# Four tiles for a mixer state, its sample load on GpSimd's queue, and two-instruction norms in a streaming encoder step

## The chip, the cores and the metric

The kernel runs on one core of one Trainium2 chip. The metric is the device time of one execution in microseconds (us). Before the change three runs took 1357.20, 1358.41 and 1359.65 us, so the median is 1358.41 us.

## What is computed

The reference is one step of a one-layer streaming encoder: 1024 frames of a new stream (the prompt) and 32 frames of a running stream (the sample), which brings its states along.

```python
def run_trunk(x, states, params):            # DEPTH = 1
    h, st_new = mixer(rms_norm(x, g_mix_pre), ...)   # GLA | HGRN2 | mLSTM heads, then cat @ w_out
    x = x + rms_norm(h, g_mix_post)
    h, ffn_buf = conv_ffn(rms_norm(x, g_ffn_pre), ...)   # gelu(gate) * val, D_FF = 2816
    x = x + rms_norm(h, g_ffn_post)
...
def rms_norm(x, g):
    y = xf * lax.rsqrt(jnp.mean(xf * xf, axis=-1, keepdims=True) + EPS)
...
    s_new = exp(b_last) * s + einsum('bjhk,bjhv->bhkv', kc * exp(b_last - b), vc)   # GLA and HGRN2, chunks of 64
```

D_MODEL is 1024, so a norm is over 1024 columns. For the prompt the states start at zero, for the sample they come from HBM (`s_gh` holds GLA's and HGRN2's matrices, 128x256, and `s_c` mLSTM's). The states after the last chunk are outputs too.

## The kernel before

The 1056 rows are nine **units**: u = 0 to 7 are 128 prompt rows each, and u = 8 is the sample's 32 rows. Each product in f32 is three TensorE matmuls of split operands (`mm3`, L101 to L103), so most TensorE rows come in threes with these lines.

The stages follow each other, and overlap at their edges:

1. The input norm and the in-projection (`pv` products), in three groups of units: 0 to 2, 3 to 5, 6 to 8. While one group is projected, the **mixers** of the group before it run piece by piece between the projection's pieces (`merge` and `pump`).
2. The mixers, in the order of units 0, 1, 2, 3, 4, 5, 8, 6, 7. A mixer makes scores (`sc`), masks them into `P` (DVE, L831), makes the outputs `og` and `oh` (heads of GLA and HGRN2) and `om` and `oi` (mLSTM) on TensorE, and `finish` (L1009 to L1019) norms them by head: ACT squares, DVE sums, GpSimd makes the reciprocal root (`hrs`), DVE multiplies it into `cat` (L1017), GpSimd multiplies the gate in (L1019).
3. The out-projection (`zp` products, by unit and half: `zp40` is unit 4, half 0), with the post norm, the residual and the FFN's pre norm (`outproj`). Its operands `ch` and `cl` are split from `ctp` transposes (L1105, L1106), and `fxt` transposes bring the normed rows into the FFN's layout (L1207, then `z` on DVE, L1212). The mixers of units 8, 6 and 7 run between the pieces of the out-projection of units 0 to 4 and 8.
4. The FFN's up products (`puw`, `pux`) and down products (`x`, `q`), by Strassen-like sums of blocks; weights such as `wu0r` and `wu22r` come by SP's queue and are split and summed in halves.
5. The tail: for units 0 to 3 the last down product `q` is added (`ca<-ca,q`, L1703), squared (ACT, L1578), multiplied by the gain (`ca<-ca,gp`, L1582), and two halves of `fr` (L1599) apply the post norm and the residual.

**The running state.** The states of GLA and HGRN2 lie in tiles of tag "S". A tag with `bufs=3` has three buffers that are handed out in turn: the fourth tile takes the first one's buffer, and whoever writes it first waits for the last reader of the tile that lay there. Unit 0 and unit 8 begin with a tile S (zeros, and for the sample a load from `s_gh`, L788); each chunk of 64 rows makes one more (L927): `S4_1` is the state of unit 4 behind its second chunk. Counting in order, S8 takes the buffer of S4_1 with three buffers; S4_1 is read by the first-chunk matmuls `og<-S` and `oh<-S` of unit 5.

```python
                sp.dma_start(S, a["s_gh"])                                   # L788
                Sn = mx.tile([128, 4, 64], F32, tag="S", ..., bufs=3)        # L927
                dve.tensor_tensor(Sn, S, dec[...]..., op=ALU.mult)           # L928
                si = dve.tensor_tensor(Sn, Sn, up, op=ALU.add)               # L929
```

**The norms over 1024 columns** come in halves. ACT squares each half and leaves its sum in one column; GpSimd adds the two columns (L1176 in `outproj`, L1585 in `down_all`), and `rstd_of` divides by 1024 and adds EPS (L221) and raises to the power −1/2 (L222): three instructions of 128x1. There are nine such norms in `outproj` (`oss`) and nine in `down_all` (`gss`). Only unit 0's input norm (L307, L308) makes two instructions of it, since its squares are taken of x/32.

**What sets the order.** Each engine works through its own queue in order. The queues are ordered at build time by the framework, which simulates the program with times of its own: an edit in one place moves instructions elsewhere that it has nothing to do with. `tc.high_priority` and `tc.issue_after` steer a few of them.

Of the kernel before, what the change touches and what calls it, by code (L numbers as in the profile page):

```python
# [8 lines left out]
F32 = mybir.dt.float32  # L9
# [3 lines left out]
AF = mybir.ActivationFunctionType  # L13
ALU = mybir.AluOpType
# [9 lines left out]
EPS = 1e-6  # L24
# [67 lines left out]
def body(ctx: ExitStack, tc: tile.TileContext, a: dict):  # L92
    nc = tc.nc
    act, dve, pool, pe, sp = nc.scalar, nc.vector, nc.gpsimd, nc.tensor, nc.sync
# [25 lines left out]
    mx = mxs.enter_context(tc.tile_pool(name="mx", bufs=1, side="left", reuse_waits="tile"))  # L120
# [37 lines left out]
    def const(name, shape, dt=F32, src=None):  # L158
        t = cp.tile(shape, dt, name=name)
        if src is not None:  # L160
            sp.dma_start(t, src)
        return t
# [29 lines left out]
    mhalf = const("mhalf", [128, 16])  # L192
# [26 lines left out]
    def rstd_of(out, ss, n, cols, width, eps=EPS):  # L219

        pool.tensor_scalar(out, ss, 1.0 / width, eps, op0=ALU.mult, op1=ALU.add)  # L221
        pool.tensor_tensor(out, out, mhalf[:n, :cols], op=ALU.pow)  # L222


    Ld = [mx.tile([128, 4, 128], F32, name=f"Ld{i}") for i in range(2)]
    Qz = [mx.tile([128, 6, 64], F32, name=f"Qz{i}") for i in range(2)]
    qz = mx.tile([128, 11, 128], F32, name="qz")
# [51 lines left out]
    def units_of(g):  # L279
        t0, pl, sl = GROUPS[g]  # L280
        us = [(t0 // 128 + i, 128 * i, 128) for i in range(pl // 128)]
        if sl:
            us.append((8, pl, sl))
        return us
# [8 lines left out]
    def scale_x(g):  # L293
        for (u, off, n) in units_of(g):
            x = x_in.pop(u, None)
            x = load_x(u) if x is None else x
            if g == 0:
                jk = mx.tile([128, 1024], BF16, tag=("gt", "cat", "k")[u], name=f"jk{u}", bufs=1)
            else:
                jk = mx.tile([128, 1024], BF16, tag="qe", name=f"jk{u}", bufs=1)  # L300
            rs = p1.tile([128, 1], F32, tag="rs", name=f"rs{u}", bufs=2)
            if u == 0:
                ss = p1.tile([128, 2], F32, name="ss0")
                hs = slice(0, 512), slice(512, 1024)
                for i, c in enumerate(hs):
                    act.activation(jk[:, c], x[:, c], AF.Square, scale=1.0 / 32, accum_out=ss[:, i:i + 1])
                pool.tensor_scalar(rs, ss[:, 0:1], ss[:, 1:2], EPS, op0=ALU.add, op1=ALU.add)  # L307
                pool.tensor_tensor(rs, rs, mhalf[:, :1], op=ALU.pow)  # L308
                for c in hs:
                    dve.scalar_tensor_tensor(x[:, c], x[:, c], rs, gx[:, c], op0=ALU.mult, op1=ALU.mult)  # L310
                xn_of[u] = x
                yield
                continue
            ss = p1.tile([128, 1], F32, tag="ss", name=f"ss{u}", bufs=2)
            with tc.issue_after(vgi[0].ins) if vgi else ExitStack():
                act.activation(jk[:n], x[:n], AF.Square, accum_out=ss[:n])
            rstd_of(rs[:n], ss[:n], n, 1, 1024)
            with tc.issue_after(vgi[1].ins) if vgi else ExitStack():
                dve.scalar_tensor_tensor(x[:n], x[:n], rs[:n], gx[:n], op0=ALU.mult, op1=ALU.mult)
            xn_of[u] = x  # L320
            yield
# [424 lines left out]
    def mixer(u, g, ci0):  # L746
        n = 128 if u < 8 else DEC
# [31 lines left out]


        if u in (0, 8):
            S = mx.tile([128, 4, 64], F32, tag="S", name=f"S{u}", bufs=3)
            C = mx.tile([128, 3, 65], F32, tag="C", name=f"C{u}", bufs=3)
            if u == 0:
                dve.memset(S, 0.0)
                dve.memset(C, 0.0)
            else:
                sp.dma_start(S, a["s_gh"])  # L788
                sp.dma_start(C, a["s_c"])
            state["S", u == 8], state["C", u == 8] = S, C  # L790

# [10 lines left out]
        with ExitStack() as behind:  # L802
            if halves:

                for ins in (kwi[0], halves[1]):
                    behind.enter_context(tc.issue_after(ins.ins))
            spread(dve, qz, lambda r, fs, psl: dve.tensor_tensor(qz[r, psl, :n], q4[r, fs, :], eb4[r, fs, :],
                                                                 op=ALU.mult), n)
# [73 lines left out]
        ss = mx.tile([128, 16], F32, tag="hss", name=f"hss{u}", bufs=2)  # L882
        rs = mx.tile([128, 16], F32, tag="hrs", name=f"hrs{u}", bufs=2)
# [31 lines left out]
        def states():  # L915
            si = None
            ups = []
            for ch, (o, m) in enumerate(chunks):
                up = small(4, 64)
                ups.append(up)  # L920
                for (f, r0, dk, vc) in HEADS:
                    soon(pe.matmul, up[r0:r0 + dk, f, :], kt2[:n, ch, 128 * f + r0:128 * f + r0 + dk], v[:n, vc:vc + 64],
                              start=True, stop=True)
            for ch, up in enumerate(ups):
                S = state["S", u == 8]
                Ss.append(S)
                Sn = mx.tile([128, 4, 64], F32, tag="S", name=f"S{u}_{ch}", bufs=3)  # L927
                dve.tensor_tensor(Sn, S, dec[:, :, ch:ch + 1].broadcast_to([128, 4, 64]), op=ALU.mult)  # L928
                si = dve.tensor_tensor(Sn, Sn, up, op=ALU.add)  # L929
                state["S", u == 8] = Sn  # L930
            return si
# [19 lines left out]
        for l0 in range(0, len(levels), 2):  # L951
            pair = [operands(c, i) for i, c in enumerate(levels[l0:l0 + 2])]
            last_pair = pair[-1][0] == levels[-1]
            if last_pair:
                z = mx.tile([128, 512], F32, tag="x", name=f"x{u}_0", bufs=NX)
# [125 lines left out]
    def outproj(p2, W, u):  # L1081

        gm, woh, wol = W[:3]
        n = 128 if u < 8 else DEC
# [6 lines left out]
        for hf in range(2):  # L1091
            if u < 7 or u == 8:
                ps = psb.tile([128, 4, 128], F32, tag="big", name=f"ctp{u}{hf}")
            else:
# [3 lines left out]
                ps = both[:, hf]  # L1098
# [3 lines left out]
            ch = p2.tile([128, 4, 128], F32R, tag="ch", name=f"ch{u}{hf}", bufs=3)  # L1102
# [15 lines left out]
        ss = pgm.tile([128, 4], F32, tag="oss", name=f"oss{u}", bufs=2)  # L1118
        cs = [slice(512 * hf, 512 * hf + 512) for hf in range(2)]
# [7 lines left out]

        def leave(ps, hf):

            act.activation(z[:n, cs[hf]], ps[:n], AF.Square, accum_out=ss[:n, hf:hf + 1])  # L1130
            act.copy(z[:n, cs[hf]], ps[:n])

        if u == RING[0]:

            pss = [bank(hf) for hf in range(2)]
            for k in range(8):
                next(W[3])
                for hf in range(2):
                    product(pss[hf], hf, k)
            z = ring[0](f"z{u}")  # L1140
            for hf in range(2):
                leave(pss[hf], hf)
            yield
        elif u in RING:

            z = ring[0](f"z{u}")
            for hf in range(2):
                ps = bank(hf)
                for k in range(8):
                    product(ps, hf, k)  # L1150
                leave(ps, hf)
                if not hf:
                    yield
        elif u == 6:
            pss = [bank(hf) for hf in range(2)]
            for k in range(8):
                for hf in range(2):
                    product(pss[hf], hf, k)
                if k == 3:
                    yield  # L1160
            z = tail[0](f"z{u}")
            for hf in range(2):
                leave(pss[hf], hf)
        else:

            pss = [bank(hf) for hf in range(2)]
            jk = jks[0]
            for hf in range(2):
                for k in range(8):
                    product(pss[hf], hf, k)  # L1170
                with tc.high_priority(offset=AHEAD):
                    kept["jk"] = act.activation(jk, pss[hf], AF.Square, accum_out=ss[:, hf:hf + 1])
        load_res(u)
        x = xr_of[u]
        yield
        pool.tensor_tensor(ss[:n, 2:3], ss[:n, 0:1], ss[:n, 1:2], op=ALU.add)  # L1176
        rstd_of(ss[:n, 3:4], ss[:n, 2:3], n, 1, 1024)
        if u == 7:
            for hf in range(2):
                dve.scalar_tensor_tensor(pss[hf], pss[hf], ss[:, 3:4], gm[:, cs[hf]], op0=ALU.mult, op1=ALU.mult)  # L1180
# [5 lines left out]
        if u == 7:  # L1186
            z = tail[0]("z7")
# [30 lines left out]
    upper, jks, kept, pgs = [], [], {}, ExitStack()  # L1218
# [314 lines left out]
    def down_all(ph, pc, begun, late):  # L1533
# [41 lines left out]

        def square_of(u, n, src, half, ss):
            jk = pc.tile([128, 512], BF16, tag="fjk", name=f"gjk{u}{half}", bufs=2)
            act.activation(jk[:n], src, AF.Square, accum_out=ss[:n, 2 + half:3 + half])  # L1578

        def norm_of(u, n, src, half, ss):  # L1580
            square_of(u, n, src, half, ss)
            dve.tensor_tensor(src, src, gp[:n, 512 * half:512 * half + 512], op=ALU.mult)  # L1582

        def scale_of(n, ss):
            pool.tensor_tensor(ss[:n, 0:1], ss[:n, 2:3], ss[:n, 3:4], op=ALU.add)  # L1585
            rstd_of(ss[:n, 1:2], ss[:n, 0:1], n, 1, 1024)

        def added(u, n, y, ss):
            scale_of(n, ss)
# [404 lines left out]
```

## Time and profile before

| | |
|---|---|
| median of three runs | 1358.41 us |
| the profiled execution | 1361.28 us |
| its span in the trace | 1359.5 us |
| mean TensorE clock granted | 0.985 |
| TensorE (PE) busy | 1310.0 us |
| ACT busy | 710.5 us |
| GpSimd (POOL) busy | 320.0 us |

All times of the trace are counted from the span's start. The profiled execution took 1361.28 us, 1.8 us more than its span, and 2.9 us more than the median. PE is TensorE, DVE is VectorE, ACT is ScalarE, POOL is GpSimd, SP is the engine whose queue issues most DMAs (SPq). In a timeline a row gives the start, the duration, the engine, the line, the operation with out<-in and its shape, and in brackets the idle time before it on its engine and who ended it. Up to about 536 us the in-projection and mixers 0 to 5 and 8 run, from there to about 640 us the out-projection with mixers 6 and 7, then the FFN to the tail, which begins where the last `q` products run (1341 us).

### The profile page before, as it was taken

Reading aid. Unit: us, or ns where it says so; the run is one execution under the profiler, and the core shown is the slowest. Engines: PE = TensorE matmul, PEld = TensorE weight load, DVE = VectorE, ACT = ScalarE, POOL = GpSimd, SP = SyncE. Lnnn points to the kernel's source line nnn. Section 1 sums busy time; section 2 is a strip of 40 time slices with the busy share of each in tenths; the row PEclk is TensorE's granted clock in tenths of the full one; section 3 lists DMA queues with packets and bytes.
Section 4 is the critical chain, followed back from the end, with each engine's and each line's share of the span. In section 5 each row is a group of like instructions: output and inputs, shape, how many; then the busy total and the mean of one; then the engine's idle time right before and its main releaser. Section 6 shows DMA issues by size and latency. Waiting matters only on the chain.

```text
span 1359.5 us, 29227 instructions
## 1 busy us (share of the span) xinstructions
PE 1310.0 (96%) x11472; PEld 1196.3 (88%) x11472; DVE 1026.2 (75%) x1921; ACT 710.5 (52%) x1362; POOL 320.0 (24%) x529
## 2 busy tenths in 40 slices
PE   7999999998999899999989999999999999999997
PEld 6999899998888887867889999999999997678885
DVE  5886559768598578876898888888888876499566
ACT  5555555464575455534754544545545545454552
POOL 4532302144031254313121112111111110010005
PEclk9999999999999989989999999999999999999998
DMA  9799868785889944554315457546365239644435
GB/s 345 244 358 367 280 229 281 264 291 181 295 252 316 316 142 144 156 168 115 129 48 180 127 140 182 143 113 180 111 155 140 90 121 398 262 161 137 147 105 124
DMA packets 126977, 269.72 MB, mean 198 GB/s; under 512 B 24167, under 2 KB 59271, under 8 KB 126759
## 3 DMA queue, kind: packets, MB, share of 16 engines
q1 hardware_dynamic: 113255, 244.91, 53.1%
q0 software_dynamic: 9072, 18.49, 7.3%
q10 hardware_dynamic: 4512, 4.46, 1.0%
q8 instruction: 90, 1.47, 0.4%
q14 instruction: 48, 0.39, 0.1%
HBM read 206.72 MB, written 86.18 MB: 215 GB/s over the span
## 4 chain that ended last, share of the span: by engine, by line
PE 60%; DVE 9%; DMA 2%; ACT 2%; issue 2%; POOL 1%; SPq 0%; DVEq 0%; POOLq 0%; ACTq 0%
PE pux L103 5%; PE pux L102 5%; PE pux L101 5%; PE puw L101 3%; PE puw L103 3%; PE puw L102 3%; PE q L101 3%; PE q L102 3%; PE q L103 3%; PE x L101 2%; PE x L102 2%; PE x L103 2%; PE puz L103 2%; PE puz L101 2%; PE puz L102 2%
## 5 line engine op out<-in xcount | busy, mean ns | idle before, releaser
L1409 DVE SCALAR_TENSOR_TENSOR y<-uu,fconv_sb,y 128x1060 f32<-128x1060 f32 x88 | 116.2, 1320 | 36.9 <-ACT y L1407 36.4
L1345 ACT COPY c<-pux 128x272 f32<-128x272 f32 (+1 forms) x132 | 49.4, 376 | 50.5 <-PE pux L103 49.7
L1407 ACT ACTIVATE y<-uu,fconv_sb 128x1060 f32<-128x1060 f32 x44 | 56.1, 1275 | 8.5 <-POOL uu L1403 7.8
L1406 POOL COPY fhalo<-uu 128x2 f32<-128x2 f32 x44 | 17.8, 404 | 179.5 <-DVE uu L1350 179.3
L103 PE MATMUL zp<-woh,cl 128*128 128x512 f32 (+1 forms) x144 | 57.8, 402 | 1.5 <-DVE cl L1106 1.5
L101 PE MATMUL zp<-woh,ch 128*128 128x512 f32 (+1 forms) x144 | 58.2, 414 | 0.8 <-ACT ch L1105 0.8
L101 PE MATMUL pv<-wt_0h,xh 128*128 128x256 f32 (+1 forms) x192 | 55.8, 290 | 2.8 <-DVE xl L334 1.8
L102 PE MATMUL zp<-wol,ch 128*128 128x512 f32 (+1 forms) x144 | 57.9, 402 | 0.0
L103 PE MATMUL pv<-wt_1h,xl 128*128 128x256 f32 (+1 forms) x192 | 55.4, 289 | 0.0
L101 PE MATMUL pv<-wt_1h,xh 128*128 128x256 f32 (+1 forms) x192 | 55.0, 286 | 0.0
L102 PE MATMUL pv<-wt_1l,xh 128*128 128x256 f32 (+1 forms) x192 | 54.7, 285 | 0.0
L103 PE MATMUL pv<-wt_0h,xl 128*128 128x256 f32 (+1 forms) x192 | 54.6, 284 | 0.0
L102 PE MATMUL pv<-wt_0l,xh 128*128 128x256 f32 (+1 forms) x192 | 54.4, 283 | 0.0
L1585 POOL TENSOR_TENSOR gss<-gss 128x1 f32<-128x1 f32 (+1 forms) x9 | 8.3, 924 | 184.6 <-ACT gjk L1578 184.6
L221 POOL TENSOR_SCALAR hrs<-hss 128x5 f32<-128x5 f32 (+3 forms) x27 | 10.9, 405 | 172.9 <-DVE hss L1015 170.4
L831 DVE COPY_PREDICATED P<-masks_sb,sc 128x352 f32<-128x352 int32 (+3 forms) x53 | 37.8, 713 | 6.3 <-PE sc L744 5.7
L101 PEld LDWEIGHTS pv<-wt_0h,xh 128*128 128x128 f32 x192 | 35.9, 187 | 4.5 <-DVE xl L334 2.3
L1019 POOL TENSOR_TENSOR cat<-cat,gt 128x320 f32<-128x320 f32 (+3 forms) x27 | 30.4, 1127 | 30.8 <-DVE cat L1017 24.7
L1403 POOL COPY uu<-uu 128x2 f32<-128x2 f32 x44 | 28.1, 638 | 38.7 <-DVE uu L1350 37.8
L101 PEld LDWEIGHTS pv<-wt_1h,xh 128*128 128x128 f32 x192 | 36.4, 190 | 0.7 <-issue 0.6
L222 POOL TENSOR_TENSOR hrs<-hrs,mhalf 128x5 f32<-128x5 f32 (+3 forms) x27 | 36.2, 1341 | 2.2
L103 PEld LDWEIGHTS pv<-wt_1h,xl 128*128 128x128 f32 x192 | 36.4, 189 | 0.3
(1742 smaller groups left out, 5326.4 us busy)
## 6 DMA issues: line engine op xcount, KB each, us to landing
wrP<-in_w_dn SPq DMA_DIRECT2D x27, 512.0 KB, 3.3
h_d<-y SPq DMA_DIRECT2D x22, 530.0 KB, 3.5
ht<-h_d SPq DMA_DIRECT2D x22, 530.0 KB, 10.2
wt_0r<-in_w_tok SPq DMA_DIRECT2D x21, 512.0 KB, 5.3
wt_1r<-in_w_tok SPq DMA_DIRECT2D x21, 512.0 KB, 6.2
ws_d<-in_w_dn POOLq DMA_DIRECT2D x20, 512.0 KB, 9.0
wrP<-ws_d SPq DMA_DIRECT2D x20, 512.0 KB, 4.3
wt_0l<-lt_d SPq DMA_DIRECT2D x14, 512.0 KB, 3.9
```

Of the source, the lines that this page charges most:

```text
L101: pe.matmul(ps, lh[0], rh[0], start=first, stop=False, **kw)
L102: pe.matmul(ps, lh[0], rh[1], start=False, stop=False, **kw)
L103: return pe.matmul(ps, lh[1], rh[0], start=False, stop=last, **kw)
L221: pool.tensor_scalar(out, ss, 1.0 / width, eps, op0=ALU.mult, op1=ALU.add)
L222: pool.tensor_tensor(out, out, mhalf[:n, :cols], op=ALU.pow)
L831: dve.copy_predicated(dst, mk.broadcast_to([n, 11, *mk.shape[2:]]), src)
L1019: pool.tensor_tensor(cat[:n, c0:c0 + 64 * nh], cat[:n, c0:c0 + 64 * nh], gt[:n, c0:c0 + 64 * nh], op=ALU.mult)
L1345: kept[name] = act.copy(t, ps)
L1403: pool.tensor_copy(u[:, GAP_P:GAP_P + 2], u[:, GAP_S - 2:GAP_S])
L1406: behind["POOL"] = pool.tensor_copy(fhalo[:, j, :], u[:, NCOL - 2:NCOL])
L1407: act.activation(y, u, AF.Identity, scale=fconv[:, j, 2:3], bias=fconv[:, j, 3:4])
L1409: dve.scalar_tensor_tensor(y, uu[i][:, s:s + NCOL], fconv[:, j, s:s + 1], y, op0=ALU.mult, op1=ALU.add)
```

## The change

1. The state tiles of tag "S" get four buffers instead of three (256 columns of f32 more in SBUF), so that S8 takes the buffer of S4_0 instead of S4_1.
2. The load of the sample's state is issued by GpSimd's queue instead of SP's.
3. All 19 norms of two halves go through a new helper with two GpSimd instructions: the squares are of x/32 (the factor is an argument of ACT's instruction), the first instruction adds both columns and EPS, the second is the power. 18 GpSimd additions of 128x1 are gone; unit 0's input norm keeps what it had.

```diff
+    def rstd_sum(out, a, b, n):
+        pool.tensor_scalar(out, a, b, EPS, op0=ALU.add, op1=ALU.add)
+        pool.tensor_tensor(out, out, mhalf[:n, :1], op=ALU.pow)
...
-            S = mx.tile([128, 4, 64], F32, tag="S", name=f"S{u}", bufs=3)
+            S = mx.tile([128, 4, 64], F32, tag="S", name=f"S{u}", bufs=4)
...
-                sp.dma_start(S, a["s_gh"])
+                pool.dma_start(S, a["s_gh"])
...
-                Sn = mx.tile([128, 4, 64], F32, tag="S", name=f"S{u}_{ch}", bufs=3)
+                Sn = mx.tile([128, 4, 64], F32, tag="S", name=f"S{u}_{ch}", bufs=4)
...
-            act.activation(z[:n, cs[hf]], ps[:n], AF.Square, accum_out=ss[:n, hf:hf + 1])
+            act.activation(z[:n, cs[hf]], ps[:n], AF.Square, scale=1.0 / 32, accum_out=ss[:n, hf:hf + 1])
...
-        pool.tensor_tensor(ss[:n, 2:3], ss[:n, 0:1], ss[:n, 1:2], op=ALU.add)
-        rstd_of(ss[:n, 3:4], ss[:n, 2:3], n, 1, 1024)
+        rstd_sum(ss[:n, 3:4], ss[:n, 0:1], ss[:n, 1:2], n)
...
-            act.activation(jk[:n], src, AF.Square, accum_out=ss[:n, 2 + half:3 + half])
+            act.activation(jk[:n], src, AF.Square, scale=1.0 / 32, accum_out=ss[:n, 2 + half:3 + half])
...
         def scale_of(n, ss):
-            pool.tensor_tensor(ss[:n, 0:1], ss[:n, 2:3], ss[:n, 3:4], op=ALU.add)
-            rstd_of(ss[:n, 1:2], ss[:n, 0:1], n, 1, 1024)
+            rstd_sum(ss[:n, 1:2], ss[:n, 2:3], ss[:n, 3:4], n)
```

The order of every engine is the same as before up to the place of about 536 us, but for the load itself. On GpSimd's queue, at the end of unit 4's mixer (`cat4` is its output tile, `hrs5` the root of unit 5's head norm), there stood:

```order
L222 TENSOR_TENSOR hrs4_5387<-hrs4_5387,mhalf_128 128x5
L1019 TENSOR_TENSOR cat4_5385<-cat4_5385,gt4_5242 128x320
L221 TENSOR_SCALAR hrs5_6151<-hss5_6150 128x6
L222 TENSOR_TENSOR hrs5_6151<-hrs5_6151,mhalf_128 128x6
L221 TENSOR_SCALAR hrs5_6151<-hss5_6150 128x5
```

and now stands:

```order
L222 TENSOR_TENSOR hrs4_5387<-hrs4_5387,mhalf_128 128x5
L1023 TENSOR_TENSOR cat4_5385<-cat4_5385,gt4_5242 128x320
L792 DMA S8_6945<-in_s_gh 128x256
L221 TENSOR_SCALAR hrs5_6151<-hss5_6150 128x6
L222 TENSOR_TENSOR hrs5_6151<-hrs5_6151,mhalf_128 128x6
```

The load stands one unit earlier, behind unit 4's last gate product and ahead of unit 5's roots; in SP's queue it stood between `v8` and a weight piece, behind the reads of unit 5.

From the place of 536 us to the FFN's first blocks the order of TensorE changes too: the matmuls of mixers 6 and 7 stand further ahead among the out-projection's. For mixer 7 (`sm7` and `sc7_4` are its scores, `zp81` the out-projection of the sample's second half, `zp40` that of unit 4, `ctp41` and `fxt30` transposes) there stood between two score pieces:

```order
L744 MATMUL sm7_8111<-ident_123,mqk7_7904 128x64
L101 MATMUL zp81_8321<-woh7_6892,ch81_8032 32x512
L102 MATMUL zp81_8321<-wol7_6900,ch81_8032 32x512
L103 MATMUL zp81_8321<-woh7_6892,cl81_8033 32x512
L1101 MATMUL ctp41_8384<-ident_123,ct4_7887 128x128 x4
L1207 MATMUL fxt30_8393<-ident_123,z3_7843 128x128 x4
L744 MATMUL sc7_4_8177<-Qz1_153,Ld1_151 64x2x32
```

and now (ten `zp80`, of which the first and the last are shown, then `ctp40`, then eight `zp81`, the same):

```order
L748 MATMUL sm7_8107<-ident_123,mqk7_7901 128x64
L103 MATMUL zp80_8128<-woh4_6889,cl81_8030 32x512
...
L103 MATMUL zp80_8128<-woh7_6892,cl81_8030 32x512
L1105 MATMUL ctp40_8243<-ident_123,ct4_7884 128x128 x4
L101 MATMUL zp81_8317<-woh0_6885,ch80_7891 32x512
...
L102 MATMUL zp81_8317<-wol2_6895,ch80_7891 32x512
L748 MATMUL sc7_4_8173<-Qz1_153,Ld1_151 64x2x32
```

So 18 `zp` products and a transpose stand there instead of three and two transposes. Behind `sc7_4` and up to mixer 7's outputs `og7` it is the other way: 16 `zp81` and `ctp41` stand there now, where 24 `zp40` and `fxt31` stood. Mixer 6 has it likewise: ahead of `og6` stood 17 `zp30` and two `fxt`, and now stand `ctp31` and the two `fxt`. At the FFN's entry all eleven halves of the weights `wu0r` and `wu22r` stand on DVE's queue ahead of the `z` and `cl` of units 4 and 6, where four of them stood behind.

In the tail DVE's order changes. With `q3i` and `gssi` of unit i, there stood:

```order
L1582 TENSOR_TENSOR ca_14584<-ca_14584,gp_14586 128x512
L1599 SCALAR_TENSOR_TENSOR fr2_16076<-ca_14584,gss2_15596,fr2_16076 128x512
L1703 TENSOR_TENSOR ca_14584<-ca_14584,q33_16083 128x512
L1599 SCALAR_TENSOR_TENSOR fr2_16076<-ca_14584,gss2_15596,fr2_16076 128x512
L1582 TENSOR_TENSOR ca_14584<-ca_14584,gp_14586 128x512
L1599 SCALAR_TENSOR_TENSOR fr3_16078<-ca_14584,gss3_15597,fr3_16078 128x512 x2
```

and now:

```order
L1585 TENSOR_TENSOR ca_14575<-ca_14575,gp_14577 128x512
L1705 TENSOR_TENSOR ca_14575<-ca_14575,q33_16073 128x512
L1601 SCALAR_TENSOR_TENSOR fr2_16066<-ca_14575,gss2_15587,fr2_16066 128x512 x2
L1585 TENSOR_TENSOR ca_14575<-ca_14575,gp_14577 128x512
L1601 SCALAR_TENSOR_TENSOR fr3_16068<-ca_14575,gss3_15588,fr3_16068 128x512 x2
```

The last unit's addition, which its square and its norm wait for, stands ahead of both halves of unit 2 now, not between them.

More of the change, by code (lines that the diff above doesn't have):

```diff
@@ L306, in scale_x @@
                     act.activation(jk[:, c], x[:, c], AF.Square, scale=1.0 / 32, accum_out=ss[:, i:i + 1])
-                pool.tensor_scalar(rs, ss[:, 0:1], ss[:, 1:2], EPS, op0=ALU.add, op1=ALU.add)
-                pool.tensor_tensor(rs, rs, mhalf[:, :1], op=ALU.pow)
+                rstd_sum(rs, ss[:, 0:1], ss[:, 1:2], 128)
                 for c in hs:
@@ L1171, in outproj @@
                 with tc.high_priority(offset=AHEAD):
-                    kept["jk"] = act.activation(jk, pss[hf], AF.Square, accum_out=ss[:, hf:hf + 1])
+                    kept["jk"] = act.activation(jk, pss[hf], AF.Square, scale=1.0 / 32, accum_out=ss[:, hf:hf + 1])
         load_res(u)
```

## The prediction, made before the changed kernel ran

> **What bounds the kernel now.** I read the page's head first, then the waits of TensorE, then the timelines around the three places that the change touches.
>
> ```profile
> PE 1310.0 (96%) x11472; PEld 1196.3 (88%) x11472; DVE 1026.2 (75%) x1921; ACT 710.5 (52%) x1362; POOL 320.0 (24%) x529
> ```
>
> TensorE is busy in 96% of the span, and the change takes no matmul away. The kernel can gain only where TensorE waits, where a wait slows the matmuls behind it, and in the tail, where TensorE has ended. POOL, the engine that loses instructions, is busy in 24%. So the 18 dropped additions are worth what they are worth on a path that TensorE or the end waits for, not their sum. The waits of TensorE between 440 and 700 us (total, times, longest):
>
> ```profile
> PE om L744 <- DVE cat L1017: 3.8, 1, 3.8
> PE sc L744 <- DVE P L831: 2.8, 1, 2.8
> PE zp L103 <- DVE cl L1106: 1.5, 1, 1.5
> ```
>
> The longest one is in unit 5's mixer. In DVE's timeline there:
>
> ```profile
> 467.15 0.35 DVE L946 TENSOR_TENSOR C<-C,dcs 128x195 f32<-128x195 f32 x1
> 473.66 0.43 DVE L928 TENSOR_TENSOR S<-S,dec 128x256 f32<-128x256 f32 x1 [6.16 <-DMA S<-in_s_gh]
> 475.33 0.48 DVE L1017 TENSOR_TENSOR cat<-oh,hrs 128x320 f32<-128x320 f32 x1
> ```
>
> The sample's state update (mixer 8, L928) stands on DVE ahead of unit 5's `cat`, and waits 6.16 us for the load. The chain that ended last names the load itself:
>
> ```profile
> 465.49 8.07 DMA S<-in_s_gh
> ```
>
> It starts only when unit 5's reads of the shared buffer are over, and takes 8.07 us. TensorE meanwhile:
>
> ```profile
> 434.46 0.80 PE L744 MATMUL om<-vm,w 64*64 64x65 f32 x20
> 435.19 0.80 PE L744 MATMUL oi<-C,mqz 128*64 128x65 f32 x20
> ...
> 470.47 0.29 PE L102 MATMUL pv<-xl,wt_1h 128*128 128x288 f32 x1
> 470.60 0.29 PE L103 MATMUL pv<-xh,wt_1l 128*128 128x288 f32 x1
> 474.70 1.08 PE L744 MATMUL om<-vm,w 64*64 64x65 f32 x20 [3.81 <-DVE cat L1017]
> 478.14 0.58 PE L101 MATMUL pv<-xh,wt_0h 128*128 128x288 f32 x1 [0.83 <-DVE gth L440]
> 478.51 0.44 PE L102 MATMUL pv<-xl,wt_0h 128*128 128x288 f32 x1
> 481.63 0.41 PE L103 MATMUL pv<-xh,wt_1l 128*128 128x288 f32 x1
> ```
>
> The reader sees two costs: the wait, and behind it `om` at 1.08 us instead of 0.80 (unit 4's) and 13 steps of 0.24 us between `pv` starts (478.51 to 481.63) where 0.13 is usual (470.47 to 470.60).
>
> **Part 1, the fourth buffer and the queue: −7.3 us.** S8 now takes a buffer whose readers ended a unit earlier, and POOL meets the load there:
>
> ```profile
> 445.10 1.02 POOL L1019 TENSOR_TENSOR cat<-cat,gt 128x320 f32<-128x320 f32 x1 [0.60 <-DVE cat L1017]
> 465.23 0.20 POOL L221 TENSOR_SCALAR hrs<-hss 128x6 f32<-128x6 f32 x1 [19.11 <-DVE hss L1015]
> ```
>
> It is issued at about 446.1 and needed at 467.5, so 21 us are there. POOL idles 19.11 us behind it, which hides the issue; without that cover the issue would delay the next `hrs`. Nothing waits behind it on POOL until 465.23. Its landing isn't in the trace for this queue; the nearest rows are 8.07 us (the same load on SP) and:
>
> ```profile
> ws_d<-in_w_dn POOLq DMA_DIRECT2D x20, 512.0 KB, 9.0
> ```
>
> Both end before 456 us. I take a landing that costs nothing; the other end is one that keeps the 6.16 us.
>
> Then DVE's S update starts at 467.5 (467.15 + 0.35). The distance from it to the `pv` at 478.14 is 4.48 us, which gives 471.98 on DVE's side (`cat<-oh` in it at 467.5 + 1.67 = 469.2). On TensorE's side `om` follows `pv` at 470.9, takes 0.73 (434.46 to 435.19) and `oi` as much, so the `pv` can start at 472.35. TensorE decides: 478.14 − 472.35 = 5.8 us. The slow steps go with the wait: 13 × 0.11 and 0.1 for the first, 1.5 us. Together **7.3 us**. What is late next: the `pv` are limited by TensorE alone up to the next mixer piece, and the load of C follows the chain. SP loses an issue and gains nothing.
>
> A rule of the Trainium skill speaks against the queue: "SBUF — State Buffer", section "Who interferes with whom", says that a DMA issued from GpSimd has its descriptors written by GpSimd, which is locked out of its port while DVE runs some two-port operations. By it, the landing could stretch (the page has about 3.1 instead of 0.62 us); no row here shows this load on that queue, and with 21 us of room the sum would be the same.
>
> A second one prices the slow steps: "TensorE: Matmul & The Clock Gate", section "What's actually happening", has the clock halve after an idle window of about 3.4 us and come back after as much work. The 3.81 us wait and the 3.5 us of slow steps behind it agree. By that rule the shorter wait of part 2 would leave no slow steps and be worth 2.8 instead of 4.7 us; its own rows, below, show slow steps.
>
> **Part 2, mixers 6 and 7 ahead in TensorE's order: −1.5 us.** Only the order moves here. The rows that decide:
>
> ```profile
> 458.04 1.78 PE L744 MATMUL mi<-v,kt 128*32 128x64 f32 x44
> ...
> 589.42 0.67 PE L744 MATMUL sc<-Qz,k 64*64 64x64 f32 x32
> ...
> 596.44 1.13 PE L744 MATMUL sc<-Qz,Ld 64*64 64x64 f32 x64 [2.78 <-DVE P L831]
> 598.96 2.91 PE L744 MATMUL mi<-v,kt 128*32 128x64 f32 x44
> 603.57 0.63 PE L103 MATMUL zp<-woh,cl 128*128 128x512 f32 x1
> 604.00 0.63 PE L101 MATMUL zp<-woh,ch 128*128 128x512 f32 x1
> ...
> 632.66 0.39 PE L102 MATMUL zp<-wol,ch 128*128 128x512 f32 x1
> 632.88 0.39 PE L103 MATMUL zp<-woh,cl 128*128 128x512 f32 x1
> ```
>
> From `sc` at 589.42 to `sc7_4` at 596.44 are 7.0 us, 2.78 of them a wait: DVE needs the 7. In the new order 15 products and a transpose more stand there (and a transpose less), 15 × 0.22 = 3.3 us, so the wait goes: −2.8. Behind it `mi` took 2.91 instead of 1.78, and about four `zp` came at 0.43 (603.57 to 604.00) instead of 0.22 (632.66 to 632.88): another −1.9, so −4.7.
>
> Against it: from `sc7_4` to `og7` DVE ends its last operand:
>
> ```profile
> 605.27 0.40 DVE L929 TENSOR_TENSOR S<-S,mi 128x256 f32<-128x256 f32 x1
> ```
>
> That is 9.2 us behind `sc7_4`. TensorE's work there, with `sc` and `mi` at full speed (1.1 and 1.0 for their two parts, 1.8), 16 × 0.22 and a transpose of about 0.5, is 8 us, so a wait of about 1.0 appears. Ahead of `og6` 17 products leave (3.7 us), by the same chain of masks and state updates; I take 1.0 there too, an estimate by `og7`. At the FFN's entry DVE has four more weight halves ahead of `cl60`; the 1.46 us wait there may grow or stay, and I put 1.2 for it (two halves of about 0.6 us). The sum is −4.7 + 3.2 = **−1.5**. Bounds: −4.7 with none of these waits, and on the other side the cover taken away in full (next but one part).
>
> **Part 3, the additions: −1.5 us, all in the tail.** The last round on POOL, and the last two on DVE:
>
> ```profile
> 1353.08 0.70 POOL L1585 TENSOR_TENSOR gss<-gss 128x1 f32<-128x1 f32 x1 [2.35 <-ACT gjk L1578]
> 1353.87 0.19 POOL L221 TENSOR_SCALAR gss<-gss 128x1 f32<-128x1 f32 x1
> ```
>
> ```profile
> 1350.85 0.74 DVE L1599 SCALAR_TENSOR_TENSOR fr<-ca,gss,fr 128x512 f32<-128x512 f32 x1
> 1351.51 0.68 DVE L1703 TENSOR_TENSOR ca<-ca,q 128x512 f32<-128x512 f32 x1
> 1354.72 1.41 DVE L1599 SCALAR_TENSOR_TENSOR fr<-ca,gss,fr 128x512 f32<-128x512 f32 x2 [1.00 <-POOL gss L222]
> ```
>
> The last `fr` waits for POOL's root. Without the addition the root starts 0.79 earlier (1353.08 to 1353.87), and the new DVE order puts the last `ca,q` ahead of a half of `fr` (0.66, 1350.85 to 1351.51): 1.45. If the first instruction of a pair is the slow one whatever it does (0.70 against 0.19), 0.5 of that stays. The other 14 additions lie beside TensorE's work, which hides them; I cost them at nothing. Where one lies on a path after all (unit 7's norm, just ahead of the FFN), it is worth up to the 0.79 above. ACT's squares keep their shape; the factor is an argument, as in unit 0's norm.
>
> **Sum.** −7.3 − 1.5 − 1.5 = −10.3 us, from 1361.28 to 1351.0 for the profiled execution. That run was 2.9 us above the median; against the median of 1358.41 the forecast is **1348.1 us**.
>
> **The rivals.**
> *The load still late.* If POOL's queue delivers more than 21 us after the issue, part 1 shrinks by what is missing, to nothing at 27.5 us: 1355.4. Against: 8.07 and 9.0 us above. For: this queue isn't seen with a busy DVE under this load. Chance 0.06.
> *Absorbed.* The in-projection runs 7 us earlier, and meets a weight or a cast row that doesn't: half to all of parts 1 and 2 goes, 1353 to 1357. For: the load itself, of 128 KB, took 8.07 us there, so the transfers do queue. Against: in the stretch of the wait the DMA engines are busy 0.54 of the time (the last column but one), so they have room to be ahead:
>
> ```profile
> 465.00:490.00 25.00, 20.19 (x184) 18.98 (x179) 13.73 (x43) 8.32 (x24) 15.21 (x21) 0.86 0.54 185
> ```
>
> Chance 0.12.
> *Slower.* TensorE reaches the mixers' pieces before DVE is done. The order takes 61 products from ahead of such pieces (17 before `og6`, 20 and 24 further on), 61 × 0.22 = 13.4 us of cover. It decides from the point where DVE is later than TensorE at three or more of these places by over 2 us each; each such wait leaves some 1.5 us of slow steps, as above. All of it lost costs 13.4 + 4.5 = 18 and gives 1358.4 − 8.8 + 18 = 1367; I put it at about 12 and 1361.5. Against: DVE is busy in 26.25 of 33 and 22.63 of 41 us there, so it has gaps to run ahead in.
>
> ```profile
> 560.00:593.00 33.00, 32.79 (x409) 22.89 (x408) 26.25 (x68) 17.41 (x42) 11.92 (x14) 1.00 0.44 135
> 593.00:634.00 41.00, 38.22 (x399) 32.11 (x396) 22.63 (x48) 11.69 (x26) 11.09 (x20) 0.92 0.48 130
> ```
>
> Chance 0.11.
> *The middle gains in full.* None of the three new waits shows: −4.7, and 1344.9. Chance 0.16.
>
> **How the numbers follow.** The forecast has 0.55 (1346 to 1351). The range 1343 to 1357 leaves out most of the slower rival and a little below the full gain. The measurement can tell about 0.2%, 2.7 us, from no change: 1355.7 and 1361.1 are the bounds. Faster: 0.55 + 0.16 + 0.09 of the absorbed + 0.03 of the late load = 0.83. Same: 0.03 + 0.03 and 0.02 of the slower case = 0.08. Slower: 0.09.
>
> **What would show it.** Right, if DVE's wait at L928 is gone, `om` stands right behind `pv` at about 471, the `pv` run at 0.13, and everything behind stands 7 us earlier up to 520. For part 2, `sc7_4` without a wait and `og6` and `og7` with one of about 1 us. For part 3, the last `fr` 1.5 us nearer to the last matmul. Wrong, if the load lands behind 467, if a wait on C or a weight takes its place, or if TensorE's waits between 536 and 700 us grow in sum.

## The result, and the profile after

The changed kernel took 1356.28 us (median of 12 runs, 1351.24 to 1362.18), the kernel before beside it 1362.57 us (12 runs, 1357.20 to 1366.56). The ratio is **0.9962, with a 95% interval of 0.9945 to 0.9979**: 5.2 us faster, between 2.9 and 7.5 (the two medians alone differ by 6.3). A second measurement (below) gave 0.9971 (0.9952 to 0.9990). The forecast was 10.3 us. The direction was right, and about half of the gain came.

The first term came as forecast. DVE's state update in the changed kernel, and the load on POOL and its landing:

```profile
470.18 0.41 DVE L932 TENSOR_TENSOR S<-S,dec 128x256 f32<-128x256 f32 x1
470.52 0.54 DVE L1021 TENSOR_TENSOR cat<-og,hrs 128x384 f32<-128x384 f32 x1
```

```profile
448.43 0.65 POOL L792 DMA_DIRECT2D S<-in_s_gh  x1
468.00 0.19 POOL L221 TENSOR_SCALAR hrs<-hss 128x6 f32<-128x6 f32 x1 [18.93 <-DVE hss L1019]
```

```profile
S<-in_s_gh POOLq DMA_DIRECT2D x1, 128.0 KB, 5.3
```

No bracket stands behind L932: the wait of 6.16 us is gone. The load landed 5.3 us behind its issue, some 16 us ahead of its need, and POOL idled 18.93 us behind it. TensorE there:

```profile
473.36 0.29 PE L103 MATMUL pv<-xh,wt_1l 128*128 128x288 f32 x1
473.58 0.80 PE L748 MATMUL om<-vm,w 64*64 64x65 f32 x20
474.31 0.80 PE L748 MATMUL oi<-C,mqz 128*64 128x65 f32 x20
475.29 0.37 PE L101 MATMUL pv<-xh,wt_0h 128*128 128x288 f32 x1 [0.18 <-PE oi L748]
475.50 0.29 PE L102 MATMUL pv<-xl,wt_0h 128*128 128x288 f32 x1
475.63 0.30 PE L103 MATMUL pv<-xh,wt_0l 128*128 128x288 f32 x1
```

`om` stands right behind `pv`, at 0.80 instead of 1.08 us, and the `pv` behind them come at 0.13. The mark at 451 us comes 3 us later than in the trace of before, though up to there both kernels have the same order but for the load; the table below shows that this varies from trace to trace.

The middle went another way than forecast. TensorE's longest waits from 530 to 700 us, before:

```profile
PE puw L101 <- ACT T1h L1258: 2.9, 1, 2.9
PE sc L744 <- DVE P L831: 2.8, 1, 2.8
PE zp L103 <- DVE cl L1106: 1.5, 1, 1.5
...
PE zp L101 <- ACT ch L1105: 0.8, 1, 0.8
...
PE ctp L1101 <- DVE z L1212: 0.4, 1, 0.4
```

and in the changed kernel:

```profile
PE puw L101 <- ACT T1h L1261: 3.0, 1, 3.0
PE ctp L1105 <- ACT z L1135: 3.0, 1, 3.0
PE zp L101 <- DVE z L1215: 1.6, 1, 1.6
PE og L748 <- DVE P L835: 1.4, 1, 1.4
PE mi L748 <- ACT kt L896: 0.9, 1, 0.9
```

Before there were 2.8 (`sc` on P) and, at the FFN's entry, 0.4, 0.75 and 1.46, with two of 0.2: 5.8 us. Now these are gone and four others stand there: 1.4, 0.9, 1.6 and 3.0, or 6.9 us. The first row of each, `puw`, belongs to the up products and is about the same in both.

For where the time went, three traces of before and four of the changed kernel, cut at the same instructions (length of the piece, us, and the difference of the means; the marks are the scores `sm` of the mixers at 451 and 498 us, a score product `sc` at 536 us just ahead of the place where the orders part, the last `zp`, the last `puw`, the last `q` and the last `fr`):

| piece | before, three traces | changed, four traces | difference |
|---|---|---|---|
| start to `sm` 451 | 450.9, 451.0, 453.7 | 454.0, 450.3, 451.2, 452.6 | +0.2 |
| to `sm` 498 (the load) | 47.6, 47.5, 45.2 | 39.4, 39.5, 40.0, 39.4 | **−7.2** |
| to `sc` 536 | 37.1, 37.1, 37.3 | 37.7, 38.2, 39.1, 38.1 | +1.1 |
| to the last `zp` (the order) | 127.4, 127.3, 127.1 | 126.7, 125.6, 127.2, 130.5 | **+0.2** |
| to the last `puw` | 458.3, 458.3, 458.3 | 458.8, 458.8, 458.8, 458.8 | +0.5 |
| to the last `q` | 227.9, 227.9, 227.9 | 229.5, 229.5, 229.8, 228.0 | +1.3 |
| to the last `fr` (the tail) | 5.55, 5.55, 5.55 | 5.01, 5.02, 5.00, 5.00 | **−0.55** |

The sum is −4.5 us, which agrees with the two timed ratios.

### The profile page after: what moved, and what is told of

Same layout as the page of the kernel before. It is cut to its first block, busy times and chain, and to the rows that moved or that the text cites. A ratio compares the mean times of both kernels' runs of the same rounds, so it can differ in the third digit from the quotient of the medians.

```text
span 1355.9 us, 29205 instructions
## 1 busy us (share of the span) xinstructions
PE 1308.5 (97%) x11472; PEld 1193.8 (88%) x11472; DVE 1027.0 (76%) x1921; ACT 710.6 (52%) x1362; POOL 315.9 (23%) x512
## 4 chain that ended last, share of the span: by engine, by line
PE 62%; DVE 9%; ACT 2%; DMA 2%; issue 1%; POOL 1%; SPq 0%; DVEq 0%; POOLq 0%; ACTq 0%
PE pux L103 5%; PE pux L102 5%; PE pux L101 5%; PE puw L103 3%; PE puw L101 3%; PE puw L102 3%; PE q L101 3%; PE q L102 3%; PE q L103 3%; PE x L101 2%; PE x L102 2%; PE x L103 2%; PE puz L101 2%; PE puz L103 2%; PE puz L102 2%; PE puy L102 2%
## 5 line engine op out<-in xcount | busy, mean ns | idle before, releaser
L227 POOL TENSOR_SCALAR gss<-gss 128x1 f32<-128x1 f32 (+1 forms) x9 | 11.8, 1306 | 188.1 <-ACT gjk L1581 188.0
```

What stands on the lines that cost most here:

```text
L227: pool.tensor_scalar(out, a, b, EPS, op0=ALU.add, op1=ALU.add)
```

## The experiments

**The load's two halves, apart and together.** `tiles_only`: `bufs=3` to `bufs=4` for tag S. `queue_only`: `sp.dma_start(S, ...)` to `pool.dma_start(S, ...)`. `state_only`: both.

> The kernel before with four buffers for tag S alone; the load stays on SP's queue. TensorE, DVE and POOL keep the order of before, and on SP the load stands one row earlier, ahead of v8 and behind q6. Theory (the buffer frees the load, the queue's place decides when it starts): it is issued about 0.6 us earlier, at 464.9 instead of 465.49, DVE's wait at L928 stays at 5 to 6 us, and the time moves by 0 to -1 us. Rival (the fourth buffer is what counts): the wait goes, -7 to -8 us. If the program's early part (before 440 us) is later than before's by 2 to 3 us in this run too, the larger buffer area moves it; by the theory it isn't.

> The kernel before with the load on GpSimd's queue alone; three buffers. The load stands behind unit 4's last gate product and has to wait there for unit 5's reads (464.6 us), and unit 5's roots hrs stand behind it on POOL; on DVE four rows of unit 5's mixer move (its two cat behind a few others). Theory: the load is issued at 464.6 to 465.3 and lands in about 5 us (as in the changed kernel), so DVE waits 2 to 4 us in place of 6.2, and the roots come 0.5 to 1 us late: -1 to -4 us. Rival (the queue alone does it): the wait goes, -7 to -8 us. Rival (blocked roots cost as much as the wait): 0 to +2 us.

> The kernel before with four buffers and the load on GpSimd's queue, the norms as before. TensorE's and DVE's orders are those of before. Theory (the trace of the changed kernel shows -8.0 us between 450 and 498 us and nothing in the middle): -8 us in the piece of 450 to 500 us, all of it kept to the end: -7 to -8.5 us in the time. Rival (absorbed later, by transfers that don't move): -8 at 500 us and less than -5 at 660 us.

Measured: `tiles_only` 0.9998 (0.9981 to 1.0014), `queue_only` 0.9986 (0.9967 to 1.0004), `state_only` 0.9965 (0.9944 to 0.9986). With four buffers on SP's queue:

```profile
475.87 0.43 DVE L928 TENSOR_TENSOR S<-S,dec 128x256 f32<-128x256 f32 x1 [6.25 <-DMA S<-in_s_gh]
```

```profile
466.16 2.33 SPq L270 DMA_DIRECT2D ct<-cat_d  x1
468.59 0.38 SPq L757 DMA_DIRECT2D q<-qkb_d  x1
469.02 0.44 SPq L788 DMA_DIRECT2D S<-in_s_gh  x1
```

The buffer was free, and the wait stayed at 6.25 us, because SP reached the load only at 469.02, later than I had put it; `ct<-cat_d` ahead of it in that queue took 2.33 us to issue. With the queue alone, POOL and DVE:

```profile
464.54 0.65 POOL L788 DMA_DIRECT2D S<-in_s_gh  x1 [19.77 <-PE oh L744]
465.26 0.20 POOL L221 TENSOR_SCALAR hrs<-hss 128x6 f32<-128x6 f32 x1
```

```profile
470.71 0.42 DVE L928 TENSOR_TENSOR S<-S,dec 128x256 f32<-128x256 f32 x1 [3.57 <-DMA S<-in_s_gh]
```

POOL itself waited 19.77 us for unit 5's reads (`oh`), with the roots behind it, and DVE waited 3.57 us. Neither half is worth much, both together take the wait away: the buffer says when the load may start, the queue's place when it does. In the trace of before the two came within a microsecond of each other: the last read of the buffer ended at 464.6 us, and SP was through with the issue ahead of the load (`v`) at 465.4. The piece from 451 to 498 us is 48.2 (`tiles_only`), 45.0 (`queue_only`) and 40.2 us (`state_only`), beside 46.7 of before. In its trace `state_only` is 8.5 us ahead at the last `zp`, so little of the load's gain is absorbed up to there; its timed gain of 4.7 us (1.9 to 7.6) is less than the 7 to 8.5 expected.

**The norms, and their two places.** `norms_only` is the changed kernel with S as before; `outproj_norms` has the new norms in the out-projection alone, `ffn_norms` in the down part alone (the squares' factor of 1/32 goes with them, not shown):

```diff
-        pool.tensor_tensor(ss[:n, 2:3], ss[:n, 0:1], ss[:n, 1:2], op=ALU.add)      # outproj_norms
-        rstd_of(ss[:n, 3:4], ss[:n, 2:3], n, 1, 1024)
+        rstd_sum(ss[:n, 3:4], ss[:n, 0:1], ss[:n, 1:2], n)
...
-            pool.tensor_tensor(ss[:n, 0:1], ss[:n, 2:3], ss[:n, 3:4], op=ALU.add)  # ffn_norms
-            rstd_of(ss[:n, 1:2], ss[:n, 0:1], n, 1, 1024)
+            rstd_sum(ss[:n, 1:2], ss[:n, 2:3], ss[:n, 3:4], n)
```

> The changed kernel with three buffers and the load on SP's queue again: the norms alone. TensorE's, DVE's and POOL's orders are those of the changed kernel. Theory (the trace of the changed kernel): nothing before 536 us, 0 in the middle (536 to 660 us: -1 to +1.5), -0.5 in the tail: -1.5 to +1 us in the time. Rival (my forecast): -1.5 in the middle and -1.5 in the tail, -3 us. Rival (the new order costs, and the changed kernel hides it behind the 8 us gained): +2 to +4 us.

> The kernel before with the two-instruction norms in the out-projection alone. TensorE's order is that of the changed kernel over the whole program, and DVE's from 536 us to the FFN; the tail's order is that of before. Theory (the nine additions there free nothing, but their going moves mixers 6 and 7 ahead): TensorE's waits between 536 and 660 us go from 5.6 us (0.2 + 2.8 + 0.4 + 0.75 + 1.46) to about 7 (og6 1.4, mi 0.9, zp 1.6, ctp 3), nothing in the tail: +1 to +2.5 us. Rival (my forecast of the middle): -1.5 us. Rival (no cost, the 1.8 us of norms_only were chance): 0.

> The kernel before with the two-instruction norms in the down part alone. TensorE's order is that of before; on DVE seven rows of the tail move. Theory: the last fr starts 5.0 us behind the last q matmul instead of 5.55, as in the changed kernel, and nothing else moves: -0.5 to -0.7 us. Rival (my forecast): -1.5 us in the tail.

Measured: 1.0013 (0.9997 to 1.0029), 1.0017 (0.9998 to 1.0035) and 0.9987 (0.9969 to 1.0005). Each interval holds 1, so the times alone decide nothing (the +1.8 us of `norms_only` lies just above what its theory allowed); the traces say more. TensorE's waits of `outproj_norms` from 530 to 700 us:

```profile
PE ctp L1106 <- ACT z L1136: 3.0, 1, 3.0
PE puw L101 <- ACT T1h L1262: 3.0, 1, 3.0
PE zp L101 <- DVE z L1216: 1.6, 1, 1.6
PE og L749 <- DVE P L836: 1.4, 1, 1.4
PE mi L749 <- ACT kt L897: 0.9, 1, 0.9
```

They are the changed kernel's: its new order of mixers 6 and 7 comes from the nine additions of the out-projection alone, and with S as before. The piece from 498 us to the last `zp` is 165.7 and 166.4 us in `norms_only` and `outproj_norms`, and 164.4 or 164.5 in the five traces that have before's order there and its wait for S (three of before, `tiles_only`, `ffn_norms`). That difference doesn't show what the order costs, since it lies ahead of 536 us, where the orders are the same: behind that mark the two take 127.1 and 127.5 us and the five 125.5 to 127.4. What it costs is worked out below. In `ffn_norms` only the tail moves, to 5.01 us.

**The load without the new order of the middle.** `state_and_ffn_norms` is the changed kernel with the out-projection's norms as before; I ran it twice, the second time beside the changed kernel. `idle_addition` is the changed kernel with one addition put back whose result nobody reads:

```diff
+        pool.tensor_tensor(ss[:n, 2:3], ss[:n, 0:1], ss[:n, 1:2], op=ALU.add)   # idle_addition
         rstd_sum(ss[:n, 3:4], ss[:n, 0:1], ss[:n, 1:2], n)
```

> Four buffers, the load on GpSimd's queue, the two-instruction norms in the down part, and the out-projection's norms with three as before, so that TensorE's and DVE's order in the middle is that of before. Theory (the order that the out-projection's norms bring costs 1 to 2.5 us): -7.5 to -8.5 us against before, 1.5 to 3 us faster than the changed kernel. Rival (the order costs nothing): the changed kernel's time, -5 us.

> The changed kernel with one idle GpSimd addition of 128x1 put back ahead of each of the out-projection's nine norms (it writes a column that nobody reads). With it the schedule of the middle goes back nearly to that of before: 7 rows of TensorE differ from before, 188 lines from the changed kernel. Theory (not the instructions but the order that their number brings costs): faster than the changed kernel by 1 to 3 us although it does more, TensorE's waits between 536 and 660 us those of before (2.8 at sc of unit 7, 0.4, 0.75 and 1.46 at the FFN's entry). Rival (the order costs nothing): the changed kernel's time or 0 to 0.5 us more.

> The kernel state_and_ffn_norms once more, beside the changed kernel. Theory: 1.5 to 3.5 us faster than the changed kernel, -7 to -9 us against before. Rival (the first measurement was lucky): within 1 us of the changed kernel.

> The changed kernel once more, as the measure of the other two. Theory: -5 to -6 us against before, by part 1 (-7.4 to -8.2), the middle's order (+2) and the tail (-0.5). Rival (my forecast): -10 us.

Measured: `state_and_ffn_norms` 0.9934 (0.9916 to 0.9952) and then 0.9962 (0.9943 to 0.9980), `idle_addition` 0.9947 (0.9928 to 0.9965), `changed_again` 0.9971 (0.9952 to 0.9990). TensorE's waits of `idle_addition`:

```profile
PE sc L748 <- DVE P L835: 2.8, 1, 2.8
PE zp L103 <- DVE cl L1110: 1.5, 1, 1.5
...
PE zp L101 <- ACT ch L1109: 0.8, 1, 0.8
PE ctp L1105 <- DVE z L1216: 0.4, 1, 0.4
```

With nine instructions more the waits of before are back (nine rows of TensorE still stand elsewhere than before, between 542 and 554 us). But the lengths alone don't separate the two orders. From the `sc` at 536 us to the last `zp` every run has the same 1257 products. The three traces of `state_only` and `state_and_ffn_norms` take 124.3, 124.4 and 123.9 us for them, `idle_addition` 125.5 and `no_gain_in_tail`, with the same middle, 127.4; the changed kernel takes 125.6 to 130.5.

What spreads them is TensorE's clock. The trace records the clock granted. In this piece it stands at half for 10.2 us in all in each trace of before and in `no_gain_in_tail`, for 3.4 us in `state_only` and `state_and_ffn_norms`, for 6.8 in `idle_addition`, and for 6.8, 3.4, 6.8 and 13.7 in the changed kernel. As an estimate of what that cost I take out half of it, where TensorE was at work. Then the eleven traces with the order of before have 121.7 to 122.7 us, and the six with the new order 123.8 to 124.3. So at the same clock the new order costs 1.8 us on average: 1.3 of waits, and 0.5 of products that take longer. In the traces of before the clock stood at half for longer than in three of the changed kernel's four, which hides most of that in the table.

The times agree without proving it. The four measurements of kernels with the load and without the new order (0.9965, 0.9934, 0.9962, 0.9947) lie below the changed kernel's two (0.9962, 0.9971) by about 2 us on average, but where both were measured side by side the intervals overlap. There `idle_addition` was 3.3 us faster than the changed kernel, where 1 to 3 were expected; `state_and_ffn_norms` was only 1.2 us faster, and against before it gained 5.2 us instead of 7 to 9; the changed kernel gained 3.9 us instead of 5 to 6. `state_and_ffn_norms` is the version I would keep: faster than before in both measurements, and by the median not slower than the changed kernel in either.

**The tail without one DVE product.** `no_gain_in_tail` is `state_and_ffn_norms` without `ca<-ca,gp` of the second half.

> The kernel state_and_ffn_norms without the product ca,gp of the second column half of units 0 to 3 (the gain of the post norm is left out there). Theory (GpSimd's small instruction does not run while a DVE instruction with two operands in SBUF runs): in the first round of the tail, where DVE has nothing else, the first instruction on gss takes 0.2 us instead of 0.79, and the last fr starts about 1 us earlier or more. Rival (the first GpSimd instruction behind idle time is slow whatever DVE does): it stays at 0.7 to 0.8 us.

The first and the last round of POOL in the tail, with the product (`state_and_ffn_norms`) and the DVE rows beside it:

```profile
1337.07 0.79 POOL L227 TENSOR_SCALAR gss<-gss 128x1 f32<-128x1 f32 x1 [5.34 <-ACT gjk L1583]
1346.40 1.18 POOL L227 TENSOR_SCALAR gss<-gss 128x1 f32<-128x1 f32 x1 [1.09 <-ACT gjk L1583]
```

```profile
1337.00 0.69 DVE L1587 TENSOR_TENSOR ca<-ca,gp 128x512 f32<-128x512 f32 x1 [0.79 <-ACT gjk L1583]
1345.41 1.41 DVE L1603 SCALAR_TENSOR_TENSOR fr<-ca,gss,fr 128x512 f32<-128x512 f32 x2
1346.74 0.68 DVE L1587 TENSOR_TENSOR ca<-ca,gp 128x512 f32<-128x512 f32 x1
```

and without it (the first, third and fourth round), where the third still has DVE's `fr` beside it:

```profile
1336.50 0.30 POOL L227 TENSOR_SCALAR gss<-gss 128x1 f32<-128x1 f32 x1 [5.35 <-ACT gjk L1583]
...
1342.00 0.83 POOL L227 TENSOR_SCALAR gss<-gss 128x1 f32<-128x1 f32 x1 [0.70 <-ACT gjk L1583]
...
1346.43 0.30 POOL L227 TENSOR_SCALAR gss<-gss 128x1 f32<-128x1 f32 x1 [2.96 <-ACT gjk L1583]
```

The small POOL instruction takes 0.30 us where DVE does nothing, and else until just behind the end of DVE's instruction (1337.86 against 1337.69, and 1347.58 against 1347.42). The last `fr` moved by 0.3 us and not by the 1 us expected (4.72 instead of 5.02 behind the last `q`): DVE's order changed too, and the last `ca,q` came later (2.15 instead of 1.56). The rival, that the first instruction behind idle time is slow, falls: here 5.35 us of idle time stand ahead of 0.30.

**More traces of both kernels,** one run of each in turn.

> The kernel before once more, for a second trace. Theory (what is left open is chance: each wait of 1 to 4 us of TensorE costs a slow stretch of about 1.6 us or none): from the sm of 451 us to the last up product the length is that of the first trace within 1 us (670.3 us), and the parts before 451 us and behind 1121 us differ by up to 3 us.

> The changed kernel, third trace. Theory (chance): from 451 to the last up product -7 to -8.5 us against before as in its two traces, and the parts outside are on average those of before. Rival (the change costs something outside): before 451 us or between 1158 and 1319 us it is 1.5 to 3 us later than before in nearly every trace.

> The kernel before, third trace, taken after one of the changed kernel. Theory (chance): 670.3 us within 1 us from 451 us to the last up product; outside of it up to 3 us of difference. Rival: the parts outside are alike in all traces of before.

> The changed kernel, fourth trace. Theory (chance): -7 to -8.5 us from 451 us to the last up product, nothing systematic outside. Rival (the change costs something outside): 1.5 to 3 us later than before's traces before 451 us or between 1158 and 1319 us.

They took 1361.15 and 1361.53 (before), 1357.67 and 1359.03 us (changed), and are in the table above. Before 451 us the kernels do not differ beyond the spread of their own traces. Of before, the length from 451 us to the last up product was 670.3, 670.2 and 667.9 us, the third outside the 1 us expected. In these two traces of the changed kernel the same length was 5.3 and 3.5 us shorter than in the first of before, in its other two 7.7 and 8.3. So both missed the band expected: they lost 1.8 and 4.1 us more than the first trace between 498 us and the last `zp`. Of the rival's second half: behind the up products three of four traces of the changed kernel are 1.5 us or more later, of before none in three, of the other kernels two in ten; the next part comes back to it.

## Why the prediction was half right

**Part 1, −7.3: right, −7.2.** The wait, the slow `om` and the slow `pv` went together, and TensorE itself was next, as worked out. The agreement to 0.1 us is luck of the mean: beside the trace that the forecast was worked out from it is −8.1, since the clock stood at half there for 6.8 us, longer than the slow `pv` show; beside the third trace of before, which reached 451 us 2.7 us later and then waited less, it is −5.6. The fear behind the first rival, a late landing on POOL's queue, did not show. Of absorption, the second rival, there is a trace: a wait of `ctp` for its `ct` load near 510 us (1.84, 0.47, 0.96 and 0.72 us in the four traces of the changed kernel, none in before). `norms_only` and `outproj_norms`, where the wait for S stayed, have it too at 1.41 and 0.98, and three traces with the early load have none, so it isn't due to the shift alone. The piece from 498 to 536 us, in which it lies, is 1.1 us longer in the mean of the changed kernel; over all traces it takes 36.7 to 39.8 us, with the early load and without.

**Part 2, −1.5: wrong, +0.2 and another +0.5 at the up products' start.** The step that failed is the 3.2 us of new waits set against the −4.7. The wait of 2.78 did go, the `mi` behind it takes 1.78 again in the first trace, and `og6` waits 1.4 (forecast 1.0). But I had allowed for waits only where the mixers' outputs need DVE. `og7` (forecast 1.0) has none; instead TensorE waits 0.9 for `kt` from ACT and 1.6 for `z` of the FFN's operands, and at the FFN's entry 3.0 in one piece for ACT, where I had put 1.2 on top of 2.6. The rows moved were the cover of those too. So by the forecast the waits were to grow by 0.4 us, and they grew by 1.2 (mean of the traces). The products themselves take 0.5 longer at the same clock, for which I had no term. And the 1.9 us for slow matmuls were no sure gain: by the estimate above the clock gave 1.5 on average, but between 3.4 gained and 1.1 lost by the trace, since in each of them it stands at half behind one or two of the new waits. This is the mechanism of the rival "slower" at a fraction of its price: four places of 0.9 to 3.0 us. The +0.5 comes with the new order too: from the last `zp` to the last `puw` all six traces that have it take 458.8 us, and those with the order of before 458.3 (`idle_addition` 459.4).

**Part 3, −1.45: right in place, wrong in size, −0.55.** From the last `q`, the last `ca,q` came 0.78 earlier (2.34 to 1.56 us behind it; forecast 0.66). The addition's 0.79 came to nothing: it had been a wait for DVE's product and not the cost of an instruction, and the next POOL instruction took it over, at 1.18. From POOL's start to the root's end the last round took 1.61 before (1353.08 to 1354.69) and 1.83 now:

```profile
1349.24 1.18 POOL L227 TENSOR_SCALAR gss<-gss 128x1 f32<-128x1 f32 x1 [1.09 <-ACT gjk L1581]
1350.51 0.56 POOL L228 TENSOR_TENSOR gss<-gss,mhalf 128x1 f32<-128x1 f32 x1
```

I had allowed for part of this, with 0.5 of the 0.79 staying; all of it stayed, and 0.2 more. The reason I gave there, that the first instruction of a pair is slow whatever it does, is not the one: alone it takes 0.30. "SBUF — State Buffer" of the Trainium skill, section "Who interferes with whom", says that a DVE instruction with two inputs in SBUF contends with a GpSimd instruction that reads SBUF. By that rule `ca,gp` (two inputs in SBUF) is what POOL waits for, and the runs agree: 0.79 beside it, 0.30 without it.

**Outside the sum,** +1.3 on average behind the up products. There the two kernels wait alike, and what differs is the clock behind the wait. The changed kernel's first trace, and its fourth:

```profile
1160.46 1.56 PE L101 MATMUL x<-P1w,P1h 128*128 128x512 f32 x4 [1.23 <-ACT P1w L107]
1161.82 0.63 PE L102 MATMUL x<-P1w,P1h 128*128 128x512 f32 x1
1162.25 0.63 PE L103 MATMUL x<-P1w,P1h 128*128 128x512 f32 x1
...
1163.95 0.63 PE L103 MATMUL x<-P1w,P1h 128*128 128x512 f32 x1
1164.38 0.45 PE L102 MATMUL x<-P1w,P1h 128*128 128x512 f32 x1
```

```profile
1163.29 1.19 PE L101 MATMUL x<-P1w,P1h 128*128 128x512 f32 x4 [1.23 <-ACT P1w L107]
1164.33 0.39 PE L102 MATMUL x<-P1w,P1h 128*128 128x512 f32 x1
1164.55 0.40 PE L103 MATMUL x<-P1w,P1h 128*128 128x512 f32 x1
```

The same wait of 1.23 us is followed by steps of 0.43 us, up to 1164.38, in one, and by steps of 0.23 in the other. The record of the clock tells the two apart. In every trace the half-rate stretches start at multiples of 3.41 us from each other and last 3.41 or 6.83 us (the one at the program's end aside), and this grid lies elsewhere in each execution. The two waits next to each other here, 0.59 and 1.23 us, are in all 17 traces. In the five with the slow stretch, 1.61 to 1.81 us of them fall into one interval of that grid, in the twelve without 0.91 to 1.63. So the place of the waits in the grid decides, and that differs between executions of one kernel. Whether the changed kernel meets the slow case more often than the others, or whether this +1.3 is chance, three of four traces don't settle.

Between the −10.3 us of the forecast and the −4.5 of the traces are 5.8 us: 1.7 in part 2 and 0.5 behind it, 0.9 in part 3, and, in places where the order did not change, 1.1 between 498 and 536 us, 1.3 behind the up products and 0.3 in the rest.

## What to carry to other kernels

A load that arrives late has two causes, the buffer that isn't free and the queue that hasn't come to it; look for both before taking one away, because each alone may give nothing. A short instruction that looks long beside another engine's can be a wait: then removing it hands the wait to the next one, so ask what it ends with. Where a scheduler orders the queues, the instructions taken away count for less than the order that comes out; compare that order, list every wait that the moved rows were covering, and try the edit without its part that moves them. Where kernels differ by 0.3%, look at how long the clock stood at half in each trace before you read a cause out of two lengths.

## What the runs showed of the hardware

- TensorE's half-rate stretches last 3.41 or 6.83 us (69 and 36 of them in the 17 traces, the one at the program's end aside) and start on a grid of 3.41 us that lies elsewhere in each execution (its first point 0.3 to 3.3 us behind the span's start). Two waits of 0.59 and 1.23 us close together are followed by one where 1.61 to 1.81 us of them fall into one interval of the grid (five traces), and by none where it is 0.91 to 1.63 us (twelve). A stretch of 3.41 us costs about 1.6 us (some eight products at 0.43 in place of 0.23). It is one reason why the same program spreads over 11 us: in the twelve runs of the changed kernel the granted clock went from 0.992 (1351.24 us) to 0.984 (1362.18 us).
- A POOL instruction on one column (`TENSOR_SCALAR gss`) took 0.30 us alone and 0.79 to 1.18 us beside DVE instructions with two inputs in SBUF, ending 0.1 to 0.2 us behind them.
- A 128 KB load issued by GpSimd's queue landed in 5.2 to 6.1 us (ten traces), of which 0.65 was the issue. On SP's queue, the DVE instruction that waited for the same load went on 8.07 us behind its issue in the trace of before, and 6.85 in `tiles_only`.
